# Recurrent heads 2 to 4 of a decoder step: v and gate by pairs of chunks with seven block products, weight factors and token sums streamed from DRAM

## The chip, the cores and the metric

The kernel runs on one NeuronCore of a Trainium2 chip. The metric is device time in microseconds (us), the median of the runs. A core has TensorE (PE, matmuls), VectorE (DVE), ScalarE (ACT) and GpSimd (POOL), each with an instruction queue of its own. SyncE (SP) starts DMA transfers, and POOL's queue starts some too. The engines meet only through semaphores: an instruction at the head of a queue that waits holds back all that stand behind it in the same queue.

## The reference

One inference step of a two-layer decoder, for 2048 prompt tokens and 32 sample tokens (8 sequences of 4), model width 1024. Layer A is gated linear attention with four heads (key width 128, value width 512), layer B windowed attention over shared keys and values. The change lies in layer A:

```python
def gla_mixer(h, state0, norm_g, w_in, w_gate2, b_gate, out_norm_g, w_out):
    u = rmsnorm(h, norm_g)
    proj = u @ w_in
    q, k, v, gate, g_low = jnp.split(proj, [...], axis=-1)
    log_a = log_sigmoid(g_low @ w_gate2 + b_gate) / A_GATE_NORMALIZER
    o, state = gla_recurrence(q * A_HEAD_DK ** -0.5, k, v, log_a, state0)
    o = rmsnorm(o, out_norm_g)
    return (o * silu(gate)) @ w_out, state
```

The recurrence goes along the tokens: the state decays by exp of the log gates, and the outer product of k and v is added; o is q times the state plus the causal part inside a chunk. Then h gets the mixer's result, and layer B runs query, gate, windowed attention with sinks, and an output product. Everything is float32.

## The kernel before

**Numbers.** A float32 operand is split into a high and a low float16 half (`split`, L187: ACT writes the high half, DVE or POOL the low one). A product is three float16 passes (`PASSES`: high·high, high·low, low·high). So 24 matmuls of 128 × 128 against 512 columns make a product with the full inner width of 1024 (8 k-tiles × 3 passes).

**Stages.** After a start, layer A's heads run one after the other, each in four blocks of 512 tokens (`Blk`, L429), each block in four chunks of 128. Layer A's output product follows (`a_out`, L1047), then the four groups of layer B's attention, then B's output product. The last already runs over pairs of chunks with seven block products in place of eight, from weight combinations that `form_steps` (L843) made and stored in DRAM during layer A.

**A block.** q and k for the whole block (`qk_steps`, 24 matmuls of 512 columns each); the decays and a tree of levels of the causal part (`level_steps`, L494); for each chunk v and gate (`vg_steps`, L472, 24 matmuls each, followed by the split of v on ACT and DVE, and by tanh and a product for the gate), then `chunk_steps` (L560): causal part, state, readout, RMS norm (POOL's `rs_m`, `rs_r`, L183/184), gating, split of the result into `ogT` (low half on POOL, L192), and a store to DRAM by SP (`ogd`, L617).

**Memory.** The normalised and transposed tokens stay in the on-chip memory in four `uT` tiles, 16 KB a partition each. Weights come through a ring of 12 `W` slots of 4 KB a partition. A head's weights are loaded at the end of the head before (`Unit.convert`, L209): SP fetches 256 KB of float32 into `wraw` (3 buffers), ACT and DVE scale and split them straight into a slot, 16 halves each for a head's v and gate together. Layer A's output weights come in the same way, into `W` slots and into `uT` slots that have come free (`wo_aside`, L924).

**Preparation.** Layer B's weights are converted early: `Unit.prepare` (L237) converts into the staging tile `pst` (2 buffers, shared with other uses), and POOL's queue stores it to DRAM (`pre`, L245), to be fetched later as one piece. These steps stand in the list `prep`; `some(n)` (L879) takes the next n of them and the block loop places them, by `PR = (1, 4, 2, 0)` to a chunk in a head's blocks. What is left over goes into the output stage.

**What sets the order.** `weave` (L148) puts the steps of two lists alternately; `behind` (L171) gives steps a lower priority. A scheduler then fixes one order for each engine and each DMA queue before the kernel runs; at run time nothing is reordered.

## Time and profile before

| | |
|---|---|
| median of 3 runs | 2835.34 us (2835.01 to 2839.59) |
| profiled execution | 2836.43 us |
| its span | 2834.6 us |
| granted TensorE clock, mean | 0.987 |
| instructions | 51373 |
| DMA moved | 395.03 MB, mean 139 GB/s |

The span runs from the first instruction to the last of the profiled execution. Engines work beside one another, so busy times do not add up to it. A group of instructions is given as line, engine, operation, destination and sources by tile name, then the total busy time and the mean of one instruction in ns, then the idle time of the engine just before them and what ended it. Under the waits, "A <- B" means that A stood idle until B had finished. PE's matmuls overlap: the duration of one is longer than the distance from one to the next.

### The profile page before, as it was taken

Reading aid. Unit: us, or ns where it says so; the run is one execution under the profiler, and the core shown is the slowest. Engines: PE = TensorE matmul, PEld = TensorE weight load, DVE = VectorE, ACT = ScalarE, POOL = GpSimd, SP = SyncE. Lnnn points to the kernel's source line nnn. Section 1 sums busy time; section 2 is a strip of 40 time slices with the busy share of each in tenths; the row PEclk is TensorE's granted clock in tenths of the full one; section 3 lists DMA queues with packets and bytes.
Section 4 is the critical chain, followed back from the end, with each engine's and each line's share of the span. In section 5 each row is a group of like instructions: output and inputs, shape, how many; then the busy total and the mean of one; then the engine's idle time right before and its main releaser. Section 6 shows DMA issues by size and latency. Waiting matters only on the chain.

```text
span 2834.6 us, 51373 instructions
## 1 busy us (share of the span) xinstructions
PE 2725.1 (96%) x19070; PEld 1390.4 (49%) x19070; DVE 1734.7 (61%) x3557; ACT 1375.5 (49%) x3241; POOL 1127.2 (40%) x1599
## 2 busy tenths in 40 slices
PE   6899999999999999999999999999999999989999
PEld 4444544444454445445344555555555555554444
DVE  5665676566657665435522665677767767777653
ACT  6554656455446543433322555566666666641110
POOL 2452234223323322115504686566657657530000
PEclk9999999999999999999999999999999999999999
DMA  8351334123312432789987576857867779798551
GB/s 212 89 126 36 101 99 154 34 86 131 123 38 86 153 97 71 177 228 269 265 192 181 116 145 129 215 114 133 179 125 132 144 167 178 151 219 168 132 120 57
DMA packets 795604, 395.03 MB, mean 139 GB/s; under 512 B 647504, under 2 KB 721176, under 8 KB 795320
## 3 DMA queue, kind: packets, MB, share of 16 engines
q1 hardware_dynamic: 782392, 356.01, 54.9%
q0 software_dynamic: 10880, 35.66, 3.5%
q8 instruction: 149, 2.44, 0.3%
q14 instruction: 103, 0.84, 0.1%
q10 hardware_dynamic: 2080, 0.07, 0.0%
HBM read 144.28 MB, written 107.54 MB: 89 GB/s over the span
## 4 chain that ended last, share of the span: by engine, by line
PE 58%; DVE 11%; ACT 10%; DMA 9%; issue 6%; POOL 5%; SPq 1%; ACTq 0%; DVEq 0%; POOLq 0%
PE pj L101 34%; PE o L101 11%; PE tr L101 8%; PE kv L101 3%; ACT o L1274 2%; DVE v L195 2%; PE lev L101 2%; DMA pre<-pst 2%; ACT v L194 1%; DVE o L1269 1%; DMA wraw<-in_a_w_in_dram 1%; POOL ogT L192 1%; DVE lev L1269 1%; DMA wraw<-in_a_w_out_dram 1%; POOL KQ L1179 1%
## 5 line engine op out<-in xcount | busy, mean ns | idle before, releaser
L101 PE MATMUL pj<-W,uT 128*128 128x512 f16 x5088 | 1198.1, 381 | 6.5 <-ACT KQ L444 2.7
L101 PEld LDWEIGHTS <-uT 128*128 128x128 f16 x6976 | 652.9, 98 | 713.6 <-issue 35.6
L101 PE MATMUL tr<-W,uT 128*128 128x512 f16 x1536 | 365.5, 379 | 0.0
L183 POOL TENSOR_SCALAR rs_m<-ss 128x1 f32<-128x1 f32 (+3 forms) x190 | 42.5, 224 | 605.0 <-ACT og L605 192.1
L101 PEld LDWEIGHTS <-X 128*128 128x128 f16 x2744 | 185.6, 98 | 142.9 <-issue 11.0
L1274 ACT ACTIVATE o<-o,mx 128x256 f32<-128x256 f32 (+1 forms) x384 | 168.6, 439 | 164.1 <-DVE mx L1269 160.1
L101 PE MATMUL pj<-uT,W 128*128 128x512 f16 (+1 forms) x912 | 188.6, 356 | 26.3 <-DMA uT<-ogT 20.8
L1269 DVE CUSTOM_DVE_ANT_0 o<-o,madd,nsink 128x256 f32<-128x256 f32 (+1 forms) x384 | 183.6, 478 | 35.4 <-PE o L101 31.3
L521 POOL TENSOR_TENSOR KQ<-KQ,bt 128x256 f32<-128x256 f32 x112 | 98.3, 877 | 259.4 <-DVE X L192 256.5
L184 POOL TENSOR_TENSOR rs_r<-rs_m,mhalf 128x1 f32<-128x1 f32 (+2 forms) x186 | 185.6, 998 | 14.1
L195 DVE SCALAR_TENSOR_TENSOR v<-o,v 128x512 f16<-128x512 f32 (+1 forms) x192 | 128.8, 671 | 97.3 <-ACT v L194 95.3
L101 PEld LDWEIGHTS <-W 128*128 128x128 f16 x2448 | 130.0, 99 | 114.2 <-issue 18.3
L101 PEld LDWEIGHTS <-v 128*128 128x128 f16 x976 | 95.5, 98 | 124.0 <-issue 7.1
L192 POOL TENSOR_TENSOR ogT<-og,ogT 128x512 f16<-128x512 f32 x68 | 82.7, 1217 | 122.3 <-ACT ogT L191 122.3
L101 PEld LDWEIGHTS <-sg 128*128 128x128 f16 x800 | 78.6, 99 | 100.8 <-DMA sg<-ogd 5.6
L191 ACT ACTIVATE X<-KQ 128x512 f16<-128x512 f32 x128 | 84.3, 659 | 84.4 <-PE lev L101 64.5
L101 PE MATMUL o<-gl,X 128*128 128x256 f16 (+1 forms) x768 | 113.4, 270 | 4.0 <-DMA gl<-KVd 2.2
L192 DVE TENSOR_TENSOR X<-KQ,X 128x512 f16<-128x512 f32 x128 | 98.0, 765 | 31.0 <-ACT X L191 26.5
L101 PE MATMUL pj<-W,v 128*128 128x512 f16 x448 | 105.3, 382 | 8.2 <-DVE st L1614 5.7
L194 ACT ACTIVATE v<-o 128x512 f16<-128x512 f32 (+1 forms) x192 | 111.3, 580 | 3.6
L1274 ACT ACTIVATE lev<-lev,mx 128x256 f32<-128x256 f32 (+1 forms) x128 | 56.5, 442 | 103.6 <-DVE mx L1269 101.5
L245 POOL DMA_DIRECT2D pre<-pst x72 | 50.3, 701 | 131.9 <-DVE pst L195 114.1
(441 smaller groups left out, 4858.2 us busy)
## 6 DMA issues: line engine op xcount, KB each, us to landing
pre<-pst POOLq DMA_DIRECT2D x72, 256.0 KB, 3.5
W<-pre SPq DMA_DIRECT2D x36, 512.0 KB
ogd<-ogT SPq DMA_DIRECT2D x68, 256.0 KB
wraw<-in_a_w_in_dram SPq DMA_DIRECT2D x64, 256.0 KB
wraw<-in_b_w_in_dram SPq DMA_DIRECT2D x64, 256.0 KB
oge<-ogT SPq DMA_DIRECT2D x64, 256.0 KB
wraw<-in_a_w_out_dram SPq DMA_DIRECT2D x32, 256.0 KB
X<-in_x_prompt_dram SPq DMA_DIRECT2D x32, 256.0 KB
```

The lines of the kernel that those rows point to most:

```text
L101: return order(nc.tensor.matmul(*a, **k))
L183: pool.tensor_scalar(m[:n, :k], ss, a, b, ALU.mult, ALU.add)
L184: pool.tensor_tensor(r[:n, :k], m[:n, :k], mhalf[:n, :k], ALU.pow)
L191: act(hi, src, AF.Copy)
L192: eng.tensor_tensor(lo, src, hi, ALU.subtract)
L194: act(hi, src, AF.Copy, scale=sc)
L195: dve.scalar_tensor_tensor(lo, src, sc, hi, ALU.mult, ALU.subtract)
L245: nc.gpsimd.dma_start(self.pre[:, :, half * 512 : half * 512 + 512], t)
L521: pool.tensor_tensor(keys, keys, d[:, :, 1:2].to_broadcast([P, NB, m]), ALU.mult)
L1179: pool.tensor_tensor(q1, q1, q2, ALU.add)
L1269: dve.tensor_tensor_reduce(pm[:, z], pm[:, z], madd.rearrange("p a b -> p (a b)")[:, (2 - nk) * P :], -0.125, nsink[:, g * GRP + h : g * G ...
L1274: act(pm[:, z], pm[:, z], AF.Exp, scale=-1.0, bias=nm_[:, h : h + 1], accum_out=bx["sum"][:, h : h + 1])
```

## The change

In heads 2 to 4, v and gate of two neighbouring chunks are made together. Call the two chunks' tokens, cut into two halves of the inner width, a 2 × 2 block matrix, and likewise the head's v and gate columns. A 2 × 2 block product by seven instead of eight multiplications needs sums of token blocks on one side and sums of weight blocks on the other:

- **Weight factors** (`Factors`): seven matrices of 512 × 512 for each head, formed from scaled weights by POOL (scaling and subtracting), split by ACT and DVE into `pst`, stored by POOL's queue into DRAM (`fa`, 4 pieces each, 84 in all). A head's factors are prepared while the head before runs, and SP fetches each as one piece of 1 MB into a ring slot.
- **Token sums** (`sum_steps`): four sums for each pair, made once by DVE (`whole`) and POOL (`add`), split by ACT and POOL, used from the slot by the first pair that needs it and stored to DRAM (`so`) for the others.
- **Products** (`pair_steps`): seven products of 12 matmuls of 512 columns into three PSUM banks X, Y and Z. After each product a step copies, adds or splits a bank. The low half of the first chunk's v moves from DVE to POOL. The order of the products is that of `FACT`.
- **Tokens**: the four `uT` tiles become eight `uP` pair tiles in the `W` ring, which now has 14 slots of 8 KB a partition and takes the place of the `uT` slots. The tokens are stored to DRAM (`uo`) during head 1 and fetched again for each block of heads 2 to 4 (24 fetches of 1 MB; 20 fetches of sums). q and k therefore run in two halves of 256 columns (`wide_steps`), and so does the low-rank gate product (`glow`).
- **Sample tokens**: their gate columns are rebuilt from three factors (12 k-tiles instead of 8). Their states are fetched and stored by fours.
- **Preparation**: layer A's output weights are prepared to DRAM and fetched by 16 loads of 512 KB in the last block. The loop places 8 factor steps (or 11 of the output weights) and `some(2)` or `some(4)` in each block of heads 2 to 4, so more of `prep` is left to the output stage.
- Scales: `SU` is 512 (was 1024); factors are scaled by 256 where weights were by 1024. Layer B's output product takes its factors and token tiles from the ring instead of from `uT` slots.

Two places show how the order moves. The first is SP's queue at the end of the third head, before. `wraw` are raw weights on their way to conversion, `ogd` the stores of the finished chunks:

```order
L617 DMA ogd_106<-ogT_9141 256x1x512
L220 DMA wraw_9358<-in_a_w_in_dram 128x512
L220 DMA wraw_9540<-in_a_w_in_dram 128x512
L220 DMA wraw_9544<-in_a_w_in_dram 128x512
L220 DMA wraw_9549<-in_a_w_in_dram 128x512
L220 DMA wraw_9553<-in_a_w_in_dram 128x512
L617 DMA ogd_107<-ogT_9457 256x1x512
```

The same place now. `fa` are the factors of head 4, `uo` the tokens and `so` the sums of its next blocks, in DRAM:

```order
L525 DMA W_10484<-fa_193 128x4096
L525 DMA W_10486<-fa_194 128x4096
L862 DMA ogd_107<-ogT_10445 256x1x512
L525 DMA W_10488<-fa_195 128x4096
L525 DMA W_10490<-fa_196 128x4096
L525 DMA W_10492<-fa_197 128x4096
L525 DMA W_10494<-fa_198 128x4096
L601 DMA W_10496<-uo_155 128x4096
L601 DMA W_10498<-uo_156 128x4096
L605 DMA W_10500<-so_162 128x4096
L862 DMA ogd_108<-ogT_10579 256x1x512
```

In place of raw weights that ACT and DVE convert on the spot, finished factors of 1 MB come one behind the other. The third to the sixth stand behind the store of a chunk's output, which waits for POOL.

The second place is POOL's queue in a block of the third head, before. `KQ` rows belong to the levels, `rs_m`, `rs_r` to the normaliser, `ogT` is a chunk's low half:

```order
L183 TENSOR_SCALAR rs_m_8504<-ss_8502 128x1
L184 TENSOR_TENSOR rs_r_8505<-rs_m_8504,mhalf 128x1
L521 TENSOR_TENSOR KQ_8251<-KQ_8251,bt_8225 128x64x4
L192 TENSOR_TENSOR ogT_8512<-og_8501,ogT_8512 128x512
L521 TENSOR_TENSOR KQ_8251<-KQ_8251,bt_8225 128x32x8
L521 TENSOR_TENSOR KQ_8251<-KQ_8251,bt_8225 128x16x16
```

A like place now, with the preparation of head 4's factors: `wraw` the scaled weights that are subtracted, `fa` the stores of the split results, `pre` a store of other weights:

```order
L479 TENSOR_TENSOR wraw_8291<-wraw_8293,wraw_8291 128x512
L479 TENSOR_TENSOR wraw_8293<-wraw_8293,wraw_8289 128x512
L484 DMA fa_195<-pst_8465 128x1024
L187 TENSOR_SCALAR rs_m_8424<-ss_8422 128x1
L188 TENSOR_TENSOR rs_r_8425<-rs_m_8424,mhalf 128x1
L196 TENSOR_TENSOR ogT_8433<-og_8421,ogT_8433 128x512
L257 DMA pre_200<-pst_8501 256x1x512
L187 TENSOR_SCALAR rs_m_8707<-ss_8705 128x1
L484 DMA fa_196<-pst_8671 128x1024
L188 TENSOR_TENSOR rs_r_8708<-rs_m_8707,mhalf 128x1
```

Subtractions and stores of staged tiles now stand between the normaliser's steps, once between its first and its second; each store waits for the DVE half of its staging tile.

The diff, cut to its core:

```diff
-NW = 12
+NW = 14
...
+    class Factors:
...
+        def part(self, m):
...
+            def scale(x):
+                k = m + 4 * (x // 2)
+                pool.tensor_scalar(b[x], b[x], gs_f[:, k : k + 1], None, ALU.mult)
+
+            def sub(x, y, z):
+                pool.tensor_tensor(b[x], b[y], b[z], ALU.subtract)
+
+            def put(n, x, eng=dve):
+                t = T("pst", [P, 2, 512], F16, 2)
+                split((t[:, 0], t[:, 1]), b[x], eng=eng)
+                nc.gpsimd.dma_start(self.d[n][:, m], t)
...
+        def fetch(self):
+            def one(n):
+                self.t[n] = T("W", [P, 4, 2, 512], F16, NW)
+                nc.sync.dma_start(self.t[n], self.d[n])
...
+    def sum_steps(q, u, put=None):
...
+            dve.tensor_tensor(t[x], v(0), v(1), ALU.add)
...
+            pool.tensor_tensor(t[x], t[y], t[z], op)
...
+            split((b["S"][:, n, :, 0], b["S"][:, n, :, 1]), t[x], eng=pool)
...
+        def wide_steps(self, w):
+
+            todo = [(z, k, n, a, b) for z in (1, 0) for k in range(KT) for n, (a, b) in enumerate(PASSES)]
...
+        def pair_steps(self, p):
...
+            def fin(n):
+                if n == 1:
+                    self.s1 = T("E", [P, 512], F32, 2)
+                    act(self.s1, bank["X"], AF.Copy, scale=vs)
+                elif n == 2:
+                    s1 = self.s1
+                    dve.scalar_tensor_tensor(s1, bank["Y"], vs, s1, ALU.mult, ALU.add)
+                    v = self.v[c0] = T("v", [P, 2, 512], F16, 4)
+                    split((v[:, 0], v[:, 1]), s1, eng=pool)
+                elif n == 6:
+                    self.sg[c0] = T("sg", [P, 512], F32, 4)
+                    act(self.sg[c0], bank["X"], AF.Copy)
+                elif n == 5:
+                    self.sg[c1] = T("sg", [P, 512], F32, 4)
+                    act(self.sg[c1], bank["Z"], AF.Copy)
+                elif n == 7:
+                    dve.tensor_tensor(self.sg[c1], bank["X"], self.sg[c1], ALU.add)
+                    silu(self.sg[c1])
+                elif n == 3:
+                    dve.tensor_tensor(self.sg[c0], bank["Z"], self.sg[c0], ALU.add)
+                    silu(self.sg[c0])
+                else:
+                    v = self.v[c1] = T("v", [P, 2, 512], F16, 4)
+                    split((v[:, 0], v[:, 1]), bank["X"], vs)
...
+            for n in FACT:
+                out += [lambda n=n, x=x: step(n, x) for x in (0, 4, 8)] + [lambda n=n: fin(n)]
...
+            more = mix(head_prep(8) if h + 1 < AH else wo_prep[j * 11 : j * 11 + 11], some(2 if h + 1 < AH else 4))
+            weave(cur.pair_steps(0), mix(prev_tail, st0 + more[: len(more) // 2]))
...
+            weave(cur.pair_steps(1), mix(mix(cur.chunk_steps(0) + cur.chunk_steps(1), lv[:4] + sparts), st1 + more[len(more) // 2 :]))
...
+            if last and nxt:
+                run(nxt.w.f.fetch())
+            if last and not nxt:
+                run(wo.steps() + wo1.steps())
```

More of the change, by code (lines that the diff above doesn't have):

```diff
@@ L145, in _body @@
     hd = [dr.tile([P, D], F32, tag=f"hd{c}", name=f"hd{c}") for c in range(NCH)]
+    uo = [dr.tile([P, KT, 2, 2 * P], F16, tag=f"uo{q}", name=f"uo{q}") for q in range(NCH // 2)]
+    so = [dr.tile([P, 4, 4, 2, P], F16, tag=f"so{q}", name=f"so{q}") for q in range(NCH // 2)]
     def weave(main, fill):
@@ L232, in load @@
         def load(self, half):
-            if self.t is None:
-                self.t = T("W", [P, 2, 1024], F16, NW)
+            self.t = self.slot.half(self.at)
             self.convert(half, lambda hl: self.t[:, hl, half * 512 : half * 512 + 512])
@@ L249, in fetch @@
         def fetch(self):
-            self.t = T("W", [P, 2, 1024], F16, NW)
+            self.t = self.slot.half(self.at)
             nc.sync.dma_start(self.t, self.pre)
@@ L319, in norm_T, with new_u, uchunk @@
                 nc.sync.dma_start(dst(hl), xt[hl][:n], transpose=True)
-    uT = [T("uT", [P, KT, 2, 512], F16, 4) for _ in range(NBL)]
+    uP = [None] * (NCH // 2)
+    def new_u(q):
+        uP[q] = T("W", [P, KT, 2, 2 * P], F16, NW)
+    def uchunk(c):
+        return uP[c // 2][:, :, :, c % 2 * P : c % 2 * P + P]
     uTs = C("uTs", [P, KT, 2, SMP], F16)
@@ new lines, in sum_steps, with whole, add, out @@
+    def sum_steps(q, u, put=None):
+        b, t = {}, {}
+        def whole(x):
+            c, kh = divmod(x, 2)
+            v = lambda hl: u()[:, kh * 4 : kh * 4 + 4, hl, c * P : (c + 1) * P]
+            dve.tensor_tensor(t[x], v(0), v(1), ALU.add)
+        def add(x, y, z, op):
+            pool.tensor_tensor(t[x], t[y], t[z], op)
+        def out(n, x):
+            split((b["S"][:, n, :, 0], b["S"][:, n, :, 1]), t[x], eng=pool)
+        def one():
+            b["S"] = T("W", [P, 4, 4, 2, P], F16, NW)
+            for x in (2, 3, 0):
+                t[x] = T("wraw", [P, 4, P], F32, 3)
+            whole(2)
+            whole(3)
+            add(3, 2, 3, ALU.add)
+            out(0, 3)
+        def two():
+            whole(0)
+            add(2, 0, 2, ALU.subtract)
+            out(2, 2)
+        def three():
+            add(3, 3, 0, ALU.subtract)
+            out(1, 3)
+        def four():
+            t[1] = t[0]
+            whole(1)
+            add(1, 1, 3, ALU.subtract)
+            out(3, 1)
+            nc.sync.dma_start(so[q], b["S"])
+            if put is not None:
+                put(b["S"])
+        return behind([one, two, three, four], 200)
@@ new lines, in u, with step @@
+        def u(self, p):
+            return self.us[p] if self.h else uP[2 * self.j + p]
+        def wide_steps(self, w):
+            todo = [(z, k, n, a, b) for z in (1, 0) for k in range(KT) for n, (a, b) in enumerate(PASSES)]
+            box = []
+            def step(part):
+                if not box:
+                    box.append(PT("pj", [P, 512], bufs=2))
+                for z, k, n, a, b in part:
+                    mm(box[0][:, z * 256 : z * 256 + 256], w(k, a), self.u(z)[:, k, b, :], start=k == 0 and n == 0, stop=k == KT - 1 and n == 2)
+            return [lambda part=todo[x : x + 8]: step(part) for x in range(0, len(todo), 8)], box
@@ L935, in _body, with head_prep, store_u @@
     sparts = []
+    wo_prep = wo.prepare() + wo1.prepare()
+    hprep = [f for h in range(1, AH) for f in facs[h].prepare()]
+    def head_prep(n):
+        out = hprep[:n]
+        del hprep[:n]
+        return out
+    def store_u(q):
+        nc.sync.dma_start(uo[q], uP[q])
     for n, (h, j) in enumerate(blocks):
@@ L1044, in _body @@
         cur = nxt
+    box_o["first"] = T("W", [P, 4, 8, P], F16, NW)
     def a_out(c):
@@ L1729, in _body @@
         if n == TOT - 1:
-            trickle += [lambda x=x: pairs[0].load(x) for x in (3, 2)] + quarters(wform_big, 1)
+            trickle += [lambda x=x: pairs[0].load(x) for x in (3, 2)] + quarters(wform, 1)
             summing += pairs[0].sums()
```

326 lines of the change are left out of this document (224 added, 102 removed).

## The prediction

> **What bounds the kernel now.** I read the totals of the engines first, then the busy time by stage, then the costliest group.
>
> ```profile
> span 2834.6 us, 51373 instructions
> PE 2725.1 (96%) x19070; PEld 1390.4 (49%) x19070; DVE 1734.7 (61%) x3557; ACT 1375.5 (49%) x3241; POOL 1127.2 (40%) x1599
> core 0: us, PE busy (x) PEld busy (x) DVE busy (x) ACT busy (x) POOL busy (x), PEclk, DMA share, GB/s
> 0.00:200.00 200.00, 160.41 (x1017) 83.79 (x1018) 121.77 (x216) 110.16 (x209) 76.96 (x131) 0.93 0.60 144
> 200.00:1170.00 970.00, 942.04 (x5990) 454.26 (x5988) 606.03 (x1036) 501.60 (x914) 293.48 (x464) 0.99 0.33 98
> 1170.00:1500.00 330.00, 321.41 (x1712) 148.98 (x1711) 132.55 (x200) 100.81 (x193) 95.47 (x137) 0.99 0.90 229
> 1500.00:2500.00 1000.00, 987.08 (x8515) 552.53 (x8513) 681.29 (x1774) 603.92 (x1804) 650.24 (x854) 1.00 0.73 150
> 2500.00:2835.00 335.00, 314.12 (x1843) 150.83 (x1841) 193.08 (x332) 59.06 (x123) 11.07 (x14) 0.97 0.60 135
> ```
>
> The rows are the start, the recurrent heads, layer A's output product, attention, and layer B's output product. TensorE (PE) is busy 942 of 970 us in the heads at a clock of 0.99: it is the bound there, and at most 28 us of waits can be won. What shortens the stage is PE work taken away. DVE stands at 62% there, ACT at 52%, POOL at 30%. The attention stage shows a fuller mixture (DVE 68%, ACT 60%, POOL 65%) with PE still at 98.7%: this is my model for a recurrent stage with more work on the other engines.
>
> **What PE loses and gains.** Prices come from runs of back-to-back matmuls in the timeline: start, length, line, count.
>
> ```profile
> 291.84 10.53 PE L101 MATMUL pj<-uT,W 128*128 128x512 f16 x48
> 1901.62 0.60 PE L101 MATMUL o<-gl,X 128*128 128x256 f16 x4
> L101 PE MATMUL pj<-W,uT 128*128 128x512 f16 x5088 | 1198.1, 381 | 6.5 <-ACT KQ L444 2.7 <-DVE sg L488 2.4 <-DVE ssg L651 0.7
> L101 PE MATMUL pj<-uTs,W 128*128 128x32 f16 (+1 forms) x1216 | 34.7, 183 | 0.0
> ```
>
> One matmul of 512 columns lasts 0.381 us, but they overlap: 48 take 10.53 us, so each further one costs (10.53 − 0.381)/47 = 0.216 us. Four of 256 columns take 0.60, with 0.270 for one alone: (0.60 − 0.27)/3 = 0.110 us. The 32-column ones cost 34.7/1216 = 0.0285 us each.
>
> - v and gate, heads 2 to 4: a pair of chunks took 2 chunks × 2 outputs × 24 = 96 matmuls of 512 columns; seven block products of 4 k-tiles × 3 passes take 84. 24 pairs × 12 × 0.216 = **−62.2 us**.
> - q and k: the tokens now lie in pair tiles of 256, so 48 matmuls of 512 become 96 of 256 in 15 blocks: 15 × (96 × 0.110 − 48 × 0.216) = **+2.9**. The low-rank gate product is split alike, 4 × (32 × 0.110 − 16 × 0.216) = **+0.3**.
> - sample tokens, three heads: the gate columns are rebuilt from three factors, 12 k-tiles where 8 were, 32 more narrow matmuls a head: 96 × 0.0285 = **+2.7**.
>
> PE's work falls by 56.3 us.
>
> **What the other engines get.** Durations of the nearest operations:
>
> ```profile
> L487 ACT ACTIVATE sg<-pj 128x512 f32<-128x512 f32 x64 | 37.6, 587 | 42.9 <-PE pj L101 42.9
> L488 DVE SCALAR_TENSOR_TENSOR sg<-sg,pj 128x512 f32<-128x512 f32 x64 | 43.5, 680 | 39.5 <-ACT sg L487 39.5
> L192 POOL TENSOR_TENSOR ogT<-og,ogT 128x512 f16<-128x512 f32 x68 | 82.7, 1217 | 122.3 <-ACT ogT L191 122.3
> L245 POOL DMA_DIRECT2D pre<-pst x56: 673/688/799, 412.5 to 1166.4; - x56
> ```
>
> The last row counts the staging stores (converted weights written to DRAM by POOL's queue): 56 before, 0.688 us each of POOL. Afterwards 84 store factors and some 61 of the others remain in the stage, 145 in all, because 32 conversions of layer A's output weights now are stored too, while about 27 later ones move into the output stage.
>
> ACT gets 3 bank copies for each of 24 pairs (72), 32 splits of token sums, 36 more splits of weights (84 for 48), less 27 moved: 113 × 0.59 = +67 us. DVE gets 3 bank additions a pair less one split (48), 32 token sums, 36 splits, less 27: 89 × 0.68 = +61. POOL gets 48 scalings, 48 subtractions, 32 additions, 32 low halves of sums and 24 of v: 184 × 1.22 = 224 us, and 89 × 0.69 = 61 for stores: 293 + 285 = 578. Over a stage of some 930 us that is DVE 72%, ACT 61%, POOL 62%, within 4 points of attention's mixture. None of it is on the path by its sum alone, so the sum has it at nothing but what the next part charges; the cover is PE's 900 us.
>
> **The waits that are added.** The staging tile has two buffers, and the work meets the recurrence in the queues:
>
> ```profile
> ACT pst L194 <- DMA pre<-pst: 24.0, 14, 4.3
> POOL pre L245 <- DVE pst L195: 49.2, 32, 3.6
> PE kv L101 <- ACT v L194: 9.7, 6, 2.9
> PE kv L101 <- DVE v L195: 3.5, 3, 1.8
> 706.05 0.72 ACT L194 ACTIVATE pst<-wraw,gsb 128x512 f16<-128x512 f32 x1 [3.17 <-DMA pre<-pst]
> ```
>
> (The first rows: who waited for whom, us in all, times, longest.) The last row is ACT standing 3.17 us for a staging buffer, with v's high half queued behind it; PE then stands for v. PE's waits for v are 13.2 us for 56 stagings, or 0.24 each. Upper bound: 89 more at that price, +21. Lower bound 0: those waits fell in bursts, and here stagings are spread, one matrix column at a time; also 48 direct conversions at the head ends go. I take **+8**, nearer the low end, because a pair's first v is complete after two of its seven products, and is not multiplied into the state before the other five are through (5 × 12 × 0.216 = 13 us). That cover also hides the low half of v on POOL (1.22 for 0.68 us). Without it each pair would show the 0.5 us difference, 24 × 0.5 = 12 us. Below nothing: if the recurrent stage came to be as full as attention, its 28 us of idle would be 930 × 1.3% = 12: −16 us.
>
> The normaliser's two POOL steps now have a staging store between them, which waits for ACT and DVE; behind it queue the output's low half, its store, and on SP's queue every fetch listed after that store. SP already waits so:
>
> ```profile
> SPq L617 <- POOL ogT L192: 305.0, 42, 22.1
> L245 POOLq EVENT_SEMAPHORE  x51: 17/17/17, 433.6 to 1166.4; - x51
> pre<-pst POOLq DMA_DIRECT2D x72, 256.0 KB, 3.5
> GB/s 92 128 129 149 201 196 235 232 200 206 259 301 236 303 217 318 301 258 351 202 283 236 245 252 290 272 318 244 219 240 184 180 154 205 201 241 118 166 366 217
> ```
>
> At the head boundary seven factors of 1 MB follow one another in as many ring slots, each free once the last pair has used it. By the last row (output stage, slices of 8.25 us) a megabyte takes 1.05 MB/366 GB/s = 2.9 us at the best rate, 4.6 us at the stage's mean of 229. A freed slot's factor is wanted after the other six products, 6 × 12 × 0.216 = 15.6 us later, and each next one 2.6 us after that: the seventh 31 us after the first slot is free, when seven loads in series at the mean rate take 32. So they just fit if SP issues them as slots come free. Bounds: 0, and all seven late, the first rival below. I take **+3**: the first of the seven can find SP still waiting for a POOL result (305/42 = 7.3 us a time).
>
> Start: the first token stores stand in SP's queue ahead of later chunks' transposes. Bounds 0 and three stores at 2.9 us, about 10; **+3**. Output stage: 27 more stagings where DMA is already 0.90 busy, at 0 to 0.24 each = 6.5, and a slower ring, up to 9; **+1**, since that stage's ACT (31%) and DVE (40%) have room. Layers' other parts keep their instructions.
>
> Sum: −56.3 + 8 + 3 + 3 + 1 = −41.3. The profiled execution is 2836.4 us (1.8 beyond its span); 1.1 above the median of 2835.3. So 2835.3 − 41.3 = **2794 us**.
>
> **A rule to weigh.** POOL's rise deserves a rule. These rows show the same kind of DVE instruction under different POOL loads:
>
> ```profile
> L192 DVE TENSOR_TENSOR qe<-KQ,qe 128x512 f16<-128x512 f32 x80 | 83.1, 1039 | 32.0 <-ACT qe L191 31.4
> L192 DVE TENSOR_TENSOR X<-KQ,X 128x512 f16<-128x512 f32 x128 | 98.0, 765 | 31.0 <-ACT X L191 26.5 <-issue 3.7
> L192 DVE TENSOR_TENSOR ogT<-wraw,X 128x512 f16<-128x512 f32 x21 | 13.9, 684 | 13.8 <-ACT X L191 13.8
> ```
>
> The first runs mostly in attention (POOL 65%), the second in the heads (30%), the third at the end (3%): 684, 765, 1039 ns. About 300 such DVE operations in the heads, each (1039 − 765) = 0.27 us longer, would add 80 us: DVE at (606 + 61 + 80)/930 = 80%. That stays under PE and leaves the sum unchanged, but makes the slower rival likelier; I give it 0.10 where 0.07 stood. The Trainium skill, "SBUF — State Buffer", section on SBUF's two separate sides, says that a VectorE instruction with two SBUF inputs and a GpSimd instruction that reads SBUF shut each other out for a whole instruction. The trace agrees in sign, 684 to 1039 ns; by the rule, too, the sum would stay as it is while both engines keep below PE.
>
> **Rivals.**
> 1. *Reloads exposed at the head boundaries.* If SP stands for POOL until the old head's last product is through, seven loads take 7 × 4.6 = 32 us beside seven products of 2.6, 18 us: 14 us bare at each of three boundaries, +42 in the sum where I have +3: about 2833. For: SP's order is fixed and it waits for POOL 305 us. Against: the order of use is the order of fetch, and the heads' DMA share is 0.33. Chance 0.10.
> 2. *Saving not showing*: the stage keeps its 970 us, since PE now waits for the level chains that the products covered (24 × 2.6 = 62 us of cover gone); with the start and output terms, +4, about 2839. For: a pair has 12 matmuls fewer to hide the same chains. Against: attention's 98.7%. Chance 0.04.
> 3. *Slower: POOL becomes the bound of the heads.* Its 578 busy us plus its standing for each staged split. Before it stood 49.2 us for 56 stores, 0.9 each; it would decide from (970 − 578)/145 = 2.7 us each, within the longest wait of 3.6 that the row shows. At 3.0 us: 578 + 435 = 1013, 43 over the old stage: **≈2880**. For: stores, scalings and v stand in one queue in order. Against: the mean is a third of the deciding price. Chance 0.10.
> 4. *Fuller*: the heads as tight as attention, −16 and no added waits: 2763 to 2770. Chance 0.05.
>
> **How the numbers follow.** Forecast 0.71 (2770 to 2822: bounds −16 and 0 on one side, 21 + 10 + 9 and a partial reload on the other), the rivals as given. The forecast and the first rival make 0.81, so the range is 2770 to 2834. A measurement of this kernel tells about 0.2%, 5.7 us, from no change: faster means below 2829.7. Faster: 0.71 + 0.05 + nine tenths of the first rival = 0.85; same: the rest of it and the second = 0.05; slower 0.10.
>
> **What would show it.** Right: 288 fewer 512-column matmuls in the heads, which end some 45 us earlier with PE at 97%; PE's waits for `W` loads only a few us; POOL near 62%. Wrong: PE standing for a factor or token load at the head boundaries (rival 1); waits for level operations in the second halves of pairs (2); PE's waits ending in POOL's v, normaliser or `fa` stores, with POOL over 90% busy or waiting (3). A total below 2770 would say that the conversions at the head ends cost more than I read.

## The result and the profile after

The changed kernel takes **2956.09 us** (median of four runs) against 2836.99 for the kernel before (four runs). The ratio is **1.0412**, with a 95% interval of 1.0391 to 1.0432: slower. One of the four runs of the changed kernel took 4755.77 us at a granted clock of 0.617, and the ratio leaves it out as a slow one. The forecast was 2794.

The totals and the mean granted clock of the changed kernel, and below them the clock row of the kernel before:

```profile
span 2954.2 us, 53505 instructions
PE 2723.0 (92%) x19662; PEld 1452.1 (49%) x19662; DVE 1907.4 (65%) x3670; ACT 1437.3 (49%) x3369; POOL 1465.0 (50%) x1887
core 0: 2954.2 us, clock 0.967
```

```profile
core 0: 2834.6 us, clock 0.987
```

PE's work fell by 56 us by the prediction's count, but its busy time by 2 (2725.1 to 2723.0), since the clock fell too: (1 − 0.967) × 2954 = 97 us of full clock are lost, where (1 − 0.987) × 2835 = 37 were. Part of that loss falls on time in which PE stood idle anyway. By the clock records of the two traces, laid over PE's matmuls, PE was busy at half clock for 61 us before and 150 after, so (150 − 61)/2 = 45 us of matmul time came back in this way. And PE's idle time rose from 109 to 231 us.

Where in the program this happened is read from events that both kernels have: ACT's first copy of a block's q or k from its bank, and the first and last store of `hd` in the output stage. The first copies for heads 2, 3 and 4 (blocks 5, 9 and 13), before, then after, and the stores of `hd`:

```profile
298.70 0.58 ACT L444 ACTIVATE KQ<-pj 128x512 f32<-128x512 f32 x1
569.04 0.60 ACT L444 ACTIVATE KQ<-pj 128x512 f32<-128x512 f32 x1 [2.08 <-PE pj L101]
843.61 0.60 ACT L444 ACTIVATE KQ<-pj 128x512 f32<-128x512 f32 x1 [2.08 <-PE pj L101]
L1062 SPq DMA_DIRECT2D hd<-E x16: 320/326/530, 1166.7 to 1491.0; - x16
```

```profile
315.62 0.58 ACT L689 ACTIVATE KQ<-pj 128x512 f32<-128x512 f32 x1
631.70 0.58 ACT L689 ACTIVATE KQ<-pj 128x512 f32<-128x512 f32 x1
933.64 0.57 ACT L689 ACTIVATE KQ<-pj 128x512 f32<-128x512 f32 x1
L1356 SPq DMA_DIRECT2D hd<-E x16: 319/327/1459, 1230.9 to 1604.4; - x16
```

The stretches between such marks, in us, are used below for every run. "Work alone" is the time before with only PE's saved v and gate matmuls taken off: 7, 8 and 9 pairs fall in the three head stretches. The new order also does 48 plain matmuls of head 4's old stretch earlier, and head 2's stretch holds as many more. The out stretch ends with the last `hd` store (1515.6 and 1625.0).

| run | to head 2 | head 2 | head 3 | head 4 | out | rest | span |
|---|---|---|---|---|---|---|---|
| before | 298.7 | 270.3 | 274.6 | 323.1 | 348.9 | 1319.0 | 2834.6 |
| work alone | 298.7 | 262.6 | 253.8 | 289.4 | 348.9 | 1319.0 | 2772.4 |
| after | 315.6 | 316.1 | 301.9 | 297.3 | 394.1 | 1329.2 | 2954.2 |

So the changed kernel lost 17 us before head 2, 54 and 48 in heads 2 and 3, 8 in head 4, 45 in the output stage and 10 behind it, all against the work alone. Head 4, which has no factors to prepare, gained most of what it should (26 of 34). Of the 110 us lost in the three heads, PE's idle time makes 76 (25 before, 101 after) and matmuls at half clock 29 (PE busy at half clock for 12 us before, 71 after). The rest, some 5, is of the size of the added narrow matmuls, which the prediction had priced.

Heads 2 and 3 before (first row) and after (second row), in the view of busy time by stretch (span, PE, PEld, DVE, ACT, POOL, clock, DMA share, GB/s):

```profile
299.00:844.00 545.00, 529.64 (x3367) 255.10 (x3366) 351.02 (x604) 287.12 (x521) 179.80 (x286) 0.99 0.32 97
```

```profile
316.00:934.00 618.00, 534.48 (x3665) 287.13 (x3663) 449.50 (x657) 315.73 (x586) 393.11 (x447) 0.94 0.54 181
```

PE went from 97% to 86% at a clock of 0.94. DVE got 53 instructions more and 98.5 us more: 351/604 = 0.581 us for one before, 449.5/657 = 0.684 now, as a mean over all kinds. The waits of PE in the changed kernel's heads, from 200 to 1230 us (who waits for whom, us in all, times, longest):

```profile
PE lev L103 <- DVE X L199: 10.1, 6, 4.4
PE kv L103 <- ACT v L198: 9.7, 4, 5.5
PE pj L103 <- ACT sg L653: 9.5, 4, 5.9
PE pj L103 <- DVE sg L658: 8.6, 6, 2.8
PE lev L103 <- DVE S L778: 8.4, 9, 2.9
PE kv L103 <- DMA ke<-X: 5.6, 2, 4.9
PE pj L103 <- DVE v L199: 5.5, 4, 4.1
PE pj L103 <- DMA W<-so: 2.6, 1, 2.6
PE pj L103 <- DMA W<-uo: 1.9, 1, 1.9
PE kv L103 <- POOL v L196: 0.6, 1, 0.6
```

All rows of that window make 113 us, against 29 before (200 to 1170 us): 56 for DVE, 46 for ACT, 5.6 for the transposed keys `ke`, 4.5 for streamed tiles, 0.6 for POOL. They are many and short, and no single one stands out. The named engine is the last link only.

### The profile page after: what moved, and what is told of

It reads as the page before. It is cut to its first block, busy times and chain, and to the rows that moved or that the text cites. A ratio compares the mean times of both kernels' runs of the same rounds, so it can differ in the third digit from the quotient of the medians.

```text
span 2954.2 us, 53505 instructions
## 1 busy us (share of the span) xinstructions
PE 2723.0 (92%) x19662; PEld 1452.1 (49%) x19662; DVE 1907.4 (65%) x3670; ACT 1437.3 (49%) x3369; POOL 1465.0 (50%) x1887
## 4 chain that ended last, share of the span: by engine, by line
PE 42%; DVE 13%; DMA 13%; POOL 11%; issue 10%; ACT 9%; SPq 1%; POOLq 0%; ACTq 0%; DVEq 0%
PE pj L103 21%; PE tr L103 10%; PE o L103 7%; DMA pre<-pst 3%; PE kv L103 2%; DMA wraw<-in_a_w_in_dram 2%; ACT o L1566 2%; DVE X L196 1%; DMA fa<-pst 1%; DVE v L199 1%; POOL ogT L196 1%; POOL wraw L476 1%; POOL pre L257 1%; ACT v L198 1%; DVE o L1561 1%
## 5 line engine op out<-in xcount | busy, mean ns | idle before, releaser
L103 PE MATMUL pj<-W,W 128*128 128x512 f16 (+2 forms) x5904 | 1227.2, 357 | 74.4 <-DMA W<-ogT 22.3
L103 PEld LDWEIGHTS <-W 128*128 128x128 f16 x9952 | 837.6, 99 | 803.8 <-issue 122.9
L103 PE MATMUL tr<-W,W 128*128 128x512 f16 x2112 | 510.5, 381 | 0.0
L188 POOL TENSOR_TENSOR rs_r<-rs_m,mhalf 128x1 f32<-128x1 f32 (+3 forms) x182 | 190.6, 1047 | 12.2
L257 POOL DMA_DIRECT2D pre<-pst x104 | 72.8, 700 | 206.4 <-DVE pst L199 184.4
L103 PE MATMUL pj<-W,v 128*128 128x512 f16 x592 | 153.8, 392 | 17.9 <-DMA v<-ogd 12.8
L103 PE MATMUL pj<-W,sg 128*128 128x512 f16 x440 | 123.0, 399 | 17.4 <-DMA sg<-ogd 16.2
L196 DVE TENSOR_TENSOR pst<-wraw,pst 128x512 f16<-128x512 f32 x84 | 75.5, 904 | 64.1 <-ACT pst L195 63.9
L199 DVE SCALAR_TENSOR_TENSOR pst<-wraw,gsb,pst 128x512 f16<-128x512 f32 x64 | 48.9, 766 | 100.7 <-ACT pst L198 100.5
L196 DVE TENSOR_TENSOR qe<-KQ,qe 128x512 f16<-128x512 f32 x80 | 88.6, 1108 | 33.8 <-ACT qe L195 33.2
```

The source lines that it names most:

```text
L103: return order(nc.tensor.matmul(*a, **k))
L188: pool.tensor_tensor(r[:n, :k], m[:n, :k], mhalf[:n, :k], ALU.pow)
L196: eng.tensor_tensor(lo, src, hi, ALU.subtract)
L199: dve.scalar_tensor_tensor(lo, src, sc, hi, ALU.mult, ALU.subtract)
L257: nc.gpsimd.dma_start(self.pre[:, :, half * 512 : half * 512 + 512], t)
```

## The experiments

Each was one execution beside one of the kernel before on the same chip (2830.8 to 2847.0 over the five sets). Those runs of one and the same kernel lie up to 16 us apart, so a difference of some 10 us in the whole of two runs of different sets is within the spread; the stretches carry more of the argument. Stretches are those of the table above; some expectations give heads 2 and 3 from marks one block earlier (317 and 304 in place of 316 and 302). The code shows the core of each edit.

**1. No factors prepared for heads 3 and 4.**

```diff
+    for h in range(2, AH):
+        facs[h].d = facs[1].d
-    hprep = [f for h in range(1, AH) for f in facs[h].prepare()]
+    hprep = facs[1].prepare()
```

> Leaves out the preparation of the factors of heads 3 and 4 (56 of 84 staged pieces, 32 scalings, 32 subtractions); these heads fetch head 2's factors, so their v and gate are not the reference's. Loads, pair products and everything else stay. Theory A (the preparation of factors, above all POOL's arithmetic and what it does to DVE, makes the loss in the heads): head 2 falls from 316 to about 285 us, head 3 from 302 to about 260, the whole by about 70, to 2885. Theory B (PE waits for the bank copies between a pair's products): only some 10 to 20 us, by emptier queues, 2935 to 2945. In both the output stage keeps its 378 us.

Measured 2880.96. Head 2 285.2, head 3 256.5, head 4 295.3: heads 2 and 3 are 76 us shorter, and head 3 is within 3 us of the work alone. The output stage does not fall (403.8, after 394.1). That is theory A as far as it names the preparation; which part of the preparation costs is not told by this run.

**2. Scalings on ACT.**

```diff
-                pool.tensor_scalar(b[x], b[x], gs_f[:, k : k + 1], None, ALU.mult)
+                act(b[x], b[x], AF.Copy, scale=gs_f[:, k : k + 1])
```

> The 48 scalings of raw weights move from POOL (1.70 us each, 76 us in the heads) to ACT. Theory A: POOL's busy time in the heads falls from 578 to about 500, DVE's two-input operations get shorter by some 20 us in sum, the whole falls by 25 to 40, to about 2920. If it is not POOL but the count of staged pieces and ACT's queue that makes PE wait: no gain, 2950 to 2970.

Measured 2934.65: 21 us less, a little under the lower end of the gain foreseen. Heads 2 and 3 are 25 us shorter, a fourth of their loss, though DVE's busy time there hardly moved (446 for 450 us).

**3. No bank copies between a pair's products.**

```diff
-                if n == 1:
-                    self.s1 = T("E", [P, 512], F32, 2)
-                    act(self.s1, bank["X"], AF.Copy, scale=vs)
...
+                elif n in (1, 6, 5):
+                    return
```

> Leaves out the three copies of a bank between a pair's products (72 ACT operations) and the sums that use them, so v of a pair's first chunk and the gates of both are not the reference's; PE no longer waits for a reader of bank X after products 1 and 6, nor of Z after product 5. Theory B: PE's waits of about 40 us for these copies and additions go, with the halved clock behind them, 40 to 60 us: about 2905. Theory A: 5 to 15 us, 2940 to 2950.

Measured 2949.06, 7 us less, as theory A had it. The trace names these copies as what PE waits for last, yet without them PE waits for something else. Theory B falls.

**4. The kernel before, with preparation left late.**

```diff
-PR = (1, 4, 2, 0)
+PR = (1, 2, 1, 0)
```

> The kernel before, with 27 of the preparation steps left from the heads to layer A's output stage, as the change does, and nothing else. Theory C (the output stage's loss of 44 us comes from those steps, whose stores crowd the DMA queues while transposes of the chunks' results wait): the output stage grows from 334 us by 25 to 45, the heads gain at most 10: 2855 to 2875. If the loss there comes from the new ring or the prepared output weights: 2830 to 2842.

Measured 2859.61 (before: 2841.75). The output stage grows from 348.9 to 380.9, heads 2 to 4 gain 9, both as theory C had it: 27 steps cost 32 us there, 1.2 each, with no pair products in the kernel.

**5. No scalings and subtractions.**

```diff
-                pool.tensor_scalar(b[x], b[x], gs_f[:, k : k + 1], None, ALU.mult)
+                pass
...
-                pool.tensor_tensor(b[x], b[y], b[z], ALU.subtract)
+                pass
```

> Leaves out POOL's scalings and subtractions in the preparation of the factors (48 and 48); the raw weights are split and stored in their place, so v and gate of heads 2 to 4 are not the reference's. All 84 staged pieces with their ACT and DVE splits and their stores stay. Theory A1 (POOL's arithmetic makes the preparation's cost): heads 2 and 3 fall from 317 and 304 to about the 294 and 255 of the run without preparation, the whole to 2885 to 2900. Theory A2 (the staged pieces make it, through the two buffers and ACT's queue): 2930 to 2955. With scalings alone moved the whole fell by 21.

Measured 2911.54, between the two theories: 45 us go, where 75 went without the preparation of heads 3 and 4.

**6. No token sums for pairs 4 to 7.**

```diff
-            nc.sync.dma_start(self.fs[p], so[2 * self.j + p])
+            nc.sync.dma_start(self.fs[p], so[(2 * self.j + p) % 4])
...
-            late = h == 1 and j > 1
+            late = False
```

> Leaves out the token sums of pairs 4 to 7 (made during head 2); their places are taken by fetches of the sums of pairs 0 to 3, so v and gate of half the tokens are not the reference's. If sums cost like the preparation (POOL 43 us, DVE 16 in head 2): head 2 falls from 317 by 25 to 40, the whole to 2915 to 2930. If they lie beside other work: 2945 to 2956.

Measured 2918.9, 37 us less, as expected in sum but not in place: head 2 fell by 13 only (303.2), and head 3, in which no sums are made, by 21 (280.4). The one fixed order of all engines changes with any such omission. Why head 3 gained is not settled.

**7 and 8. POOL work added to the kernel before**, wide arithmetic or many tiny steps, in heads 2 and 3:

```diff
+            pool.tensor_scalar(b[0], b[0], gs_a[:, 0:1], None, ALU.mult)
+            pool.tensor_tensor(b[0], b[0], b[0], ALU.subtract)
```

```diff
+            pool.tensor_scalar(m[:, :1], mhalf[:, :1], 0.0, 2.0, ALU.mult, ALU.add)
+            for _ in range(5):
+                pool.tensor_tensor(r[:, :1], m[:, :1], mhalf[:, :1], ALU.pow)
```

> The kernel before with POOL arithmetic added in heads 2 and 3: in each of 9 chunks a head two loads of raw weights into the three raw buffers, each scaled and subtracted from itself by POOL on 128x512 float32 operands, some 55 us of POOL a head; nothing uses the result. Theory A1: heads 2 and 3 grow by 12 to 25 us each from 272 and 275, DVE's operations on two on-chip operands get longer. If POOL's arithmetic only fills idle POOL time: 0 to 4 each.

> As before_pool, with the same loads, but POOL's time filled by operations on one element a partition (one scaling, five powers for each load, about as long in sum). If what costs is the delay of POOL's queue: heads 2 and 3 grow as with the wide arithmetic. If it is the sharing of the on-chip memory with DVE: 0 to 5 each, and DVE's durations stay as before.

Measured 2845.86 and 2859.87 (before: 2846.99). The wide arithmetic cost 3 and 4 us a head (273.3, 278.8), the tiny steps 12 and 8 (282.0, 282.1). The first lies in the range of "only fills idle POOL time", not in that of theory A1. The second fits neither of its two cases: the heads grew by more than with the wide arithmetic, while DVE's durations stayed. So a longer POOL queue can cost by itself. The groups of DVE by line show what the wide arithmetic does all the same. Before, with wide arithmetic, and with tiny steps, over heads 2 and 3:

```profile
L195 DVE SCALAR_TENSOR_TENSOR pst<-wraw,gsb,pst 128x512 f16<-128x512 f32 x32 | 24.8, 780 | 21.2 <-ACT pst L194 21.1
L195 DVE SCALAR_TENSOR_TENSOR v<-pj,v 128x512 f16<-128x512 f32 x32 | 21.9, 686 | 8.7 <-ACT v L194 8.6
```

```profile
L195 DVE SCALAR_TENSOR_TENSOR pst<-wraw,gsb,pst 128x512 f16<-128x512 f32 x32 | 32.3, 1011 | 26.7 <-ACT pst L194 26.7
L195 DVE SCALAR_TENSOR_TENSOR v<-pj,v 128x512 f16<-128x512 f32 x32 | 21.9, 686 | 5.8 <-ACT v L194 5.7
```

```profile
L195 DVE SCALAR_TENSOR_TENSOR pst<-wraw,gsb,pst 128x512 f16<-128x512 f32 x32 | 26.0, 812 | 23.0 <-ACT pst L194 22.8
L195 DVE SCALAR_TENSOR_TENSOR v<-pj,v 128x512 f16<-128x512 f32 x32 | 21.9, 685 | 7.7 <-ACT v L194 7.5
```

The same DVE instruction on on-chip tiles (`pst<-wraw`) takes 780, 1011 and 812 ns. The one that reads a PSUM bank (`v<-pj`) stays at 686. That is the lengthening by itself, in the group that shows it most; another group on two on-chip tiles, `X<-KQ,X`, went only from 758 to 768.

**9. One product of each pair made twice**, in the changed kernel:

```diff
-                out += [lambda n=n, x=x: step(n, x) for x in (0, 4, 8)] + [lambda n=n: fin(n)]
+                out += [lambda n=n, x=x: step(n, x) for x in ((0, 4, 8) if n != 5 else (0, 4, 8, 0, 4, 8))] + [lambda n=n: fin(n)]
```

> One of the seven products of each pair is made twice into the same bank, which puts PE back at 96 matmuls of 512 columns a pair; the output is unchanged. If PE's work still sets the time of heads 2 to 4: +62 (24 x 12 x 0.216), to 3015. If waits for the other engines set it and the saving is therefore not on the path: +10 to +30, to 2965 to 2985.

Measured 2990.0, +34, between the two ranges. For 18.1, 20.7 and 23.3 us of added PE work (7, 8 and 9 pairs), head 2 took 12 more (328.1), head 3 took 8 less (294.1), head 4 took 29 more (326.3). In heads 2 and 3 together 39 us of PE work cost 4: PE's work does not set their time. In head 4 it does.

**10 to 12. Less and less preparation; and preparation added to the kernel before.** The first two lines are added to run 1, so that more of the other steps are placed early; "free" also leaves out the sums as run 6 does; the last two lines are added to run 7's work:

```diff
-            more = mix(head_prep(8) if h + 1 < AH else wo_prep[j * 11 : j * 11 + 11], some(2 if h + 1 < AH else 4))
+            more = mix(head_prep(8) if h + 1 < AH else wo_prep[j * 11 : j * 11 + 11], some(6 if h + 1 < AH else 4))
...
+            split((t[:, 0], t[:, 1]), b[0])
+            nc.gpsimd.dma_start(spare, t)
```

> The run without the preparation of heads 3 and 4, with 32 more of the other preparation steps placed in heads 2 and 3 (6 a block for 2), so fewer are left to the output stage. Theory C: that stage falls from 404 us to 360 to 370; since plain staged pieces cost little where POOL's arithmetic is gone, heads 2 and 3 grow by 0 to 12 in sum: 2835 to 2855. If staged pieces by themselves stop PE: heads grow by 20 or more, 2860 to 2880.

> The run before this one in the list, and also without the token sums of pairs 4 to 7 (their places taken by fetches of the sums of pairs 0 to 3); results of heads 2 to 4 are not the reference's. All pair products, all streams of factors, tokens and sums stay. If preparation and sums are the whole of the loss in the heads: heads 2 and 3 together at 505 to 520 us (547 before, less two times 20.7), the whole at 2795 to 2820. If the pairs' own chain (banks, streams) loses as well: heads 2 and 3 together above 535.

> The kernel before with whole preparation steps added in heads 2 and 3: in each of 9 chunks a head two loads of raw weights, each scaled and subtracted by POOL, split by ACT and DVE into the staging tile, and stored by POOL's queue (18 a head), beside the unchanged 24 matmuls for v and gate of each chunk. POOL's arithmetic alone added 3 and 4 us a head here. If the preparation costs as much without pair products: heads 2 and 3 grow by 20 to 35 each. If it needs the pairs (fewer matmuls to hide behind, banks that wait for readers): 5 to 12 each.

Measured 2850.56, 2835.08 and 2871.15 (before: 2839.69). The output stage falls from 403.8 to 356.3 for 32 steps, heads 2 and 3 grow by 14: theory C, at 1.5 us a step. "Free" gives heads 2 and 3 287.0 and 257.9, or 551 together from the earlier marks, which is in the range of the other theory (above 535), and the whole is 15 us over the first: the loss before head 2 (313.2) and in it was still there. Preparation added to the kernel before costs 12 and 14 us a head (282.7, 289.1), between both theories.

**13 and 14. Least preparation**, and in the changed kernel the arithmetic without splits and stores:

```diff
-            for m in range(4):
+            for m in range(1):
...
-                nc.sync.dma_start(self.t[n], self.d[n])
+                for m in range(4):
+                    nc.sync.dma_start(self.t[n][:, m], self.d[n][:, 0])
...
+            nc.sync.dma_start(self.fs[p], so[0])
```

```diff
+                if self.h > 1:
+                    return
                 t = T("pst", [P, 2, 512], F16, 2)
```

> All preparation is cut to its least: one of the four pieces of each factor of head 2 is made and used four times over by heads 2 to 4, and the token sums of pair 0 stand for all; results of heads 2 to 4 are not the reference's. Pair products, streams of factors (in four loads each), tokens and sums, stores of tokens, and 32 more of the other preparation steps in heads 2 and 3 stay. If preparation and sums are all that ate the saving: the end of head 1 and its boundary, still 37 us too long in the run without heads 3 and 4's factors and half the sums, fall back, and the whole comes to 2785 to 2805, which is the forecast's own sum. If the streams or the pairs' chain of banks eat part: 2815 to 2835.

> For heads 3 and 4 POOL's scalings and subtractions stay, and the splits into the staging tile and the stores go (56 pieces); these heads fetch head 2's factors, so their results are not the reference's. Without arithmetic the whole fell by 45, without both by 75. If the two parts simply add: 30 less than the changed kernel, 2922 to 2930. If either alone is nearly covered and only both together stop PE: 45 to 70 less, 2885 to 2910.

Measured 2824.22 (before: 2830.82) and 2888.2. With least preparation the stretches are 300.0, 273.1, 262.4, 300.9 and 356.4: the losses before head 2 and in heads 2 and 3 are mostly gone, though the whole lies in the range of the other theory. Without splits and stores heads 2 and 3 are 60 us shorter, without arithmetic (run 5) 44, without either (run 1) 76. The two are not additive: leave out either, and most of what the preparation costs goes.

**15. An attempt at a better kernel:** run 2 with 10 steps a block for 4 in head 4.

```diff
-some(2 if h + 1 < AH else 4)
+some(2 if h + 1 < AH else 10)
```

> The changed kernel with the scalings on ACT and 24 more of the other preparation steps placed in head 4 (10 a block for 4), where pairs run without factors to prepare; the output is the reference's. Theory C: the output stage falls from 396 by about 30, head 4 grows by 0 to 8, the whole from 2934 to 2905 to 2912: still slower than the kernel before. If head 4 is as crowded as heads 2 and 3: 2920 to 2935.

Measured 2919.64: the output stage fell by 33 to 363.8, and head 4 grew by 24, from 297.8 to 322.1. The whole is 15 us below run 2, where 22 to 29 were foreseen, and 0.4 under the other theory's range of 2920 to 2935. Only 33 − 24 = 8 us of it come from the two stages that the edit touches; the rest is within the spread of single runs. Head 4 had less room than thought. It is faster than the changed kernel and slower than the one before (2830.82); so no version that leaves nothing out beats the kernel before here.

**16 and 17. Least preparation without bank copies, and with a product twice** (the edits of runs 3 and 9 made on run 13):

> The run with least preparation, and also without the three bank copies between a pair's products and the sums that use them. With least preparation the heads still lacked 26 us of the saving; PE's waits for these copies and additions were 17 us there, with halved clock behind some. If the bank copies are what remains: 2800 to 2808. If the streams or the start remain: 2815 to 2825.

> The run with least preparation, with one product of each pair made twice, as in the earlier run on the changed kernel, where heads 2 and 3 took 4 more and 8 less. If PE sets the time again once preparation is gone: 18 to 22 more for each of heads 2 and 3, and 55 to 65 for the whole, 2880 to 2888. If the pairs' chain of waits sets it even then: 20 to 45 for the whole, 2845 to 2868.

Measured 2825.2 and 2888.2 (before: 2840.93). Leaving out the copies gains nothing that shows here either (heads 2 and 3 take 540 us for 535); that expectation failed. The doubled product costs 64 us (62 worked out from PE's price): 17, 24 and 24 in the three heads. With preparation at its least, PE sets the time again and pays each matmul.

**One reading for all.** Over heads 2 and 3, from the view of busy time by stretch, with the length taken from mark to mark, for all runs:

| run | length | PE | DVE busy | ns for one DVE instruction |
|---|---|---|---|---|
| before | 545 | 97% | 351 (64%) | 581 |
| before_late | 541 | 98% | 337 (62%) | 578 |
| before_pool | 552 | 96% | 373 (67%) | 617 |
| before_pow | 564 | 96% | 355 (63%) | 588 |
| bare | 535 | 95% | 358 (67%) | 584 |
| bare_nocopy | 540 | 94% | 361 (67%) | 591 |
| bare_double5 | 576 | 95% | 357 (62%) | 585 |
| free | 545 | 94% | 373 (68%) | 601 |
| noprep34 | 541 | 94% | 378 (70%) | 628 |
| noprep34_early | 556 | 93% | 400 (72%) | 629 |
| noput | 558 | 92% | 393 (70%) | 652 |
| before_prep | 572 | 94% | 406 (71%) | 634 |
| noarith | 573 | 91% | 408 (71%) | 626 |
| nosum | 584 | 90% | 418 (72%) | 654 |
| fix | 587 | 89% | 447 (76%) | 682 |
| scale_act | 592 | 89% | 446 (75%) | 682 |
| nocopy | 603 | 88% | 452 (75%) | 689 |
| after | 618 | 86% | 450 (73%) | 684 |
| double5 | 622 | 90% | 445 (72%) | 677 |

Five of its rows, word for word: bare, bare_double5, before_prep, noput, double5.

```profile
300.00:835.00 535.00, 509.98 (x3698) 283.70 (x3696) 358.16 (x613) 295.08 (x540) 207.45 (x301) 0.99 0.55 177
```

```profile
300.00:876.00 576.00, 548.48 (x3879) 302.27 (x3877) 357.31 (x611) 296.04 (x538) 202.03 (x301) 0.99 0.52 165
```

```profile
300.00:872.00 572.00, 534.98 (x3369) 255.06 (x3368) 405.81 (x640) 307.27 (x557) 305.05 (x395) 0.99 0.40 126
```

```profile
315.00:873.00 558.00, 514.63 (x3671) 282.91 (x3670) 392.93 (x603) 287.94 (x532) 359.98 (x393) 0.97 0.52 176
```

```profile
316.00:938.00 622.00, 557.24 (x3837) 301.83 (x3836) 445.17 (x658) 319.44 (x587) 394.78 (x449) 0.97 0.54 183
```

From about 373 us on, the length rises with DVE's busy time (373 busy and 545 long in "free", 450 and 618 in the changed kernel), with pairs or without, and DVE's share is 67 to 76%. Added PE work costs little there (after and double5). Below that PE sets the length (bare and bare_double5). This suggests that in these heads DVE, in a chain with ACT and PE, is full at a little over 70%. It is a reading, and not shown as the cause: no run changed DVE's time alone, and the five runs with 445 to 452 us of DVE are 587 to 622 us long. The two shortest of these five have the scalings on ACT and POOL at 324 us, where the other three have it at 393 to 396. The tiny POOL steps (355 busy, 564 long) lie off the line too, so a delay by POOL's queue is a rival that no run rules out.

## Why the prediction was wrong

**PE's work was priced rightly.** 0.216 us a matmul is what the doubled product cost where PE was the bound (64 measured, 62 worked out), and head 3 without preparation (run 1) reached the work alone within 3 us.

**The step that failed is "none of it is on the path by its sum alone", with the attention stage as its model.** Attention has DVE at 68% with PE at 98.7%, and I took 72% in the heads as nearly the same. In the heads PE fell to 86% with DVE at 73%, and the added work was on the path: without the preparation of heads 3 and 4 the two heads are 76 us shorter (run 1), and 39 us of PE work put back cost 4 (run 9) but 41 once the preparation was at its least (run 17). That the work as a whole does this is shown; that DVE is the engine that is full is the reading above. Two things went into it:

- *DVE's durations.* The counts held (80 more DVE instructions from 200 to 1230 us than in the stage before, where 89 were counted), the prices did not. I put 61 us more on DVE over the whole stage, and it got 738 − 606 = 132. Heads 2 and 3 alone got 98. Compared form by form, instructions that both kernels have grew by 53 us in sum there, about half of it; the rest is the added instructions, which are wider than the mean. The same group on two on-chip tiles, before and after, and then two groups of one size in the changed kernel, the gate's sum from a bank and its last product on two on-chip tiles:

```profile
L192 DVE TENSOR_TENSOR X<-KQ,X 128x512 f16<-128x512 f32 x64 | 48.5, 758 | 14.4 <-ACT X L191 10.4 <-issue 3.7
```

```profile
L196 DVE TENSOR_TENSOR X<-KQ,X 128x512 f16<-128x512 f32 x64 | 63.7, 995 | 10.4 <-ACT X L195 9.1 <-POOL v L196 1.1
L658 DVE TENSOR_TENSOR sg<-pj,sg 128x512 f32<-128x512 f32 x15 | 10.3, 687 | 10.1 <-PE pj L103 9.9
L640 DVE SCALAR_TENSOR_TENSOR sg<-E,sg 128x512 f32<-128x512 f32 x30 | 27.4, 912 | 7.0 <-ACT E L639 6.9
```

  758 against 995 ns, and 687 against 912, with POOL at 64%. `v<-pj`, which reads a bank, stayed at 684. POOL's new arithmetic is not the whole reason: without it `X<-KQ,X` still takes 987 ns (the row below, run 5), and with least preparation 833.

```profile
L196 DVE TENSOR_TENSOR X<-KQ,X 128x512 f16<-128x512 f32 x64 | 63.2, 987 | 12.3 <-ACT X L195 12.0
```

  The rule that I weighed worked out at 80 us for DVE, in all heads; I then let it change a chance by 0.03, since 80% was "under PE". The rule of the Trainium skill, "SBUF — State Buffer", section on the two separate sides, by which a VectorE instruction with two SBUF inputs and a GpSimd instruction that reads SBUF shut each other out, agrees in sign with runs 7 and 8: 780 to 1011 ns beside wide arithmetic, 686 unchanged with one operand in PSUM. That the tiny steps, with more POOL time in sum (110 us for 102), leave 812 ns is a difference that this rule does not name.

- *The clock.* Waits were priced at their own length. But PE's clock stood at 0.94 in heads 2 and 3, and 45 of the 56 us of work saved came back as matmuls at half clock, 29 of them in heads 2 to 4.

**Staging, +8.** The term spoke of PE's waits per staged piece. Run 1 shows that the preparation of heads 3 and 4 alone costs 76 us in heads 2 and 3, and runs 5 and 14 that neither its arithmetic nor its splits and stores make that by themselves. No run changed the number of staging buffers, so their share stays open.

**Output stage, +1 with a bound of 9.** Mis-sized: it was 45. The upper bound took PE's waits for v in the heads, but what comes late here is the transposed load of a chunk's result. PE's waits after (1440 to 1610 us) and before (1340 to 1480):

```profile
PE pj L103 <- DMA sg<-ogd: 15.5, 7, 4.9
PE pj L103 <- DMA v<-ogd: 12.8, 4, 6.9
```

```profile
PE pj L101 <- DMA sg<-ogd: 4.3, 2, 3.8
PE pj L101 <- DMA v<-ogd: 2.6, 2, 2.0
```

```profile
1475.00:1600.00 125.00, 103.40 (x438) 43.71 (x437) 82.62 (x86) 47.29 (x90) 74.29 (x97) 0.89 1.01 278
```

The last row is the changed kernel between 1475 and 1600 us, with DMA at 1.01 and PE at 83%. A full DMA does not stop PE by itself: before, from 1300 to 1350 us, DMA stood at 1.04 with PE busy throughout. What PE waited for here is the transposed load. The prediction quoted DMA at 0.90 in this stage, and still wrote that ACT and DVE had room. Runs 4 and 10 put a step left for this stage at 1.2 to 1.5 us, so 27 steps make 32 to 40 of the 45.

**Start, +3.** 17 us were lost before head 2; with least preparation 1, with the token stores still in SP's queue. So it was the sums and factors made in head 1.

**Other parts, at nothing.** The stretch behind the output stage is 10 us longer (1329.2 for 1319.0). It lies between 1321 and 1331 in the other runs with pairs, and its cause is open.

**Reloads, +3, and the first rival.** That PE would hardly wait for streamed tiles was right: 4.5 us. (In the prediction's chances, nine tenths of this rival count as faster, though its 2833 lies above the bound of 2829.7; nothing in the account hangs on that slip.) At the boundary to head 2 another, smaller transfer was late beside them. The transposed keys `ke` kept PE waiting, with one load of sums behind:

```profile
374.49 0.61 PE L103 MATMUL kv<-v,ke 128*128 128x512 f16 x1 [4.87 <-DMA ke<-X]
380.12 4.64 PE L103 MATMUL pj<-W,W 128*128 128x512 f16 x12 [2.59 <-DMA W<-so]
```

**The slower rival** had POOL's queue as the bound from 2.7 us of standing for each store, and 2880. POOL's busy time came out near its forecast (596 us from 200 to 1230 us for 578). In heads 2 and 3 it was at 64%. It stood 0.8 us a store (120 us for some 145 stores from 200 to 1230 us), no more than before, and PE waited 0.6 us for it as the last link. So the sign was right and the condition was not met. A part of the loss may still come by POOL, through DVE's durations (run 7) or through delays in its queue (run 8). "Saving not showing" came true in heads 2 and 3 (run 9); that it came through the added work and not through shorter cover is what run 17 shows.

**Left open.** With least preparation the three head stretches are still 31 us over the work alone. PE's idle time makes 22 of them and matmuls at half clock 5; the rest is of the size of the added narrow matmuls. Neither the bank copies (run 16) nor waits for streamed tiles (3 us) explain the idle time. That part of PE's saving was not found.

## What to carry to other kernels

A saving on the bound engine is bought with work on the others, and a stage takes that work only up to a point that another stage's mixture does not tell: add the work first without the saving, or double the saved instruction afterwards, and see whether the time moves. Price an operation by its duration under the load that will stand beside it, not under today's: DVE on two on-chip tiles took up to 30% longer beside wide POOL arithmetic (780 to 1011 ns). Work left over by a full stage is not gone, and lands where its own resource, here DMA, may already be full.

## What the hardware showed that I had not expected

Short waits of PE cost up to half their length again: in heads 2 to 4 the stretches at half clock rose from 14 to 92 us in sum, (92 − 14)/2 = 39 us of lost clock, as PE's waits in the heads rose from 29 to 113. Each stretch is 3.4 us long or a small multiple of it (up to 13.7); the longest lies over the boundary to head 2, from 370 to 384 us, where the waits of 4.87 and 2.59 us stand. The Trainium skill, "TensorE: Matmul & The Clock Gate", Part 1, has the half clock after an idle window of about 3.4 us; the lengths agree with such a window. But the window need not be idle. By the clock records all 14 stretches of the changed kernel's heads 2 to 4 begin on one grid of 3.41 us, and in the 3.41 us before each PE had been busy for 0 to 51%, in 9 of them for 30% or more; the lowest share in a window that kept its clock is 46%. In the last window of each stretch PE was busy for 86 to 100%. So here less than 2 us of idle time inside one such window could halve the clock.
